# Four projections of a decoder layer in fp32: streaming the weights past stationary activations, with some blocks done in seven products

## The chip, the cores and the metric

The kernel runs on one core of a Trainium2 chip. The time is that of the device, in microseconds (us), from one launch. The engines are named as the profile names them: PE is TensorE (matmuls), PEld its weight loads, DVE is VectorE, ACT is ScalarE, POOL is GpSimd and SP is SyncE, which issues most transfers.

## The reference, cut to what matters

One layer of a hybrid decoder, 256 positions of 2048 channels, all in float32:

```
h = RMSNorm(x)
[q|k|v|lru_x|lru_gate|sc_B|sc_C|sc_x|merge_gates] = h @ W_in
A = causal attention of 8 heads, with a relative-position bias
B = RG-LRU(conv4(lru_x)) * gelu(lru_gate)
C = sc_B * conv3(sc_C * sc_x)
m = sig(g_A) * (A @ W_A) + sig(g_B) * (B @ W_B) + sig(g_C) * (C @ W_C)
x = x + m @ W_out
x = x + relu(RMSNorm(x) @ W_up)^2 @ W_down ;  final RMSNorm
```

`lru_gate`, `sc_B`, `sc_C` and `sc_x` are each 1024 columns wide. The change is about these four products and what stands beside them.

## The kernel before, in words

**Products in three parts.** Each float32 operand is cut into `hi`, its rounding to the matmul's type fp32r, and `lo`, what is left. A product is hi·hi + hi·lo + lo·hi. For weights, `in_parts` (L158) makes the cut for every 256 rows by 512 columns: ACT writes `hi` (L161), DVE subtracts to get `lo` (L162). Such a piece is a *step*. `ahead` (L165) puts the transfer and the cut of a step into the program LOOK = 3 steps before its use; there are 8 buffers for raw weights and 5 each for `hi` and `lo`.

**Two ways to run a product.** `group` (L245, entries `"ws"` of `order`) keeps the weights stationary and streams the activations: for each 128x128 piece of weights one matmul of 512 columns (`hi` against h's hi and lo side by side, L253) and one of 256 columns (`lo` against h's hi, L254). The result is transposed, channels on partitions; `total` (L351) adds its halves. 1024 columns of W_in take two groups, that is 16 steps, 128 matmuls of 512 and 128 of 256 columns. `pair` (L273, entries `"as"`) keeps the activations stationary and streams 512 columns of weights (L300): 16 steps, 192 matmuls of 512 columns for 1024 columns of W_in. Its result has positions on partitions.

**Blocks of quarters.** A pair can do some of its row blocks as a 2x2 scheme with seven products in place of eight (two row quarters by two column halves of the weights, two halves of the positions). `as_sequence` (L50) writes the order of the steps: `("s", m, ...)` is product m of a block, 6 matmuls; `("n", ...)` an ordinary step, 12 matmuls. A block takes 42 matmuls where ordinary steps take 48. It needs sums of weight quarters (four more DVE additions of 128x1024 for each block, L194), seven cuts in place of four, sums of the activations (`sums`, L94, kept in `hm` for h), and a few copies and additions of the results (`step`, L304; `other` in the evictions). NB_GATE = 2 blocks out of 4 for the gate projections `gt`, 0 for `v` and `y`, 1 for `up`.

**The order of the work.** SP's transfers are in the order of the program text; the order on the other engines is set by the tile framework's scheduler, which works from the program's order. `xr`, `q`, `k` run as groups, then `v` as a pair, then `sc` and `sx` as groups, then for each of three branches a pair `gt` and a pair `y`, twice; ahead of the second branch stands the group `sb` (function `second_factor`), ahead of the third the group `gr` (`recurrent_gate`). Smaller work is put between: `side` holds generators (`prepare`, `recurrence`, `attention`, `h_sums`), `after` holds single functions, and `a_bit` runs one function of `after` and `n` pieces of `side`. `finish` empties both; it is called ahead of the first `gt` and ahead of every `y`. GpSimd has a few tensor operations: the cut of the bias blocks `rb` (L464, L465), two multiplications in the recurrence (L516, L529), one in the gate's gelu (L675), and it issues small transfers.

Of the kernel before, what the change touches and what calls it, by code (L numbers as in the profile page):

```python
# [12 lines left out]
P = 128  # L13
# [54 lines left out]
def trunk_kernel(ctx, tc, x8, xn, pv, rows, w_in, rel, onehot, w_a, lru_w, w_l, w_s, w_out, w_up, w_down, out2):  # L68
# [53 lines left out]

    order = [("ws", w_in, g, 0, 8, 0) for g in (6, 7, 0, 1, 2, 3)]
    order.append(("as", w_in, 4, 0, 8, NB_V))
    for br, (w, gs) in enumerate(((w_a, (12, 13, 14, 15)), (w_s, (10, 11)), (w_l, (8, 9)))):
        order += [("ws", w_in, g, 0, 8, 0) for g in gs]
        for pair in range(2):
            order.append(("as", w_in, 16 + 4 * GATE[br] + 2 * pair, 0, 8, NB_GATE))
            order.append(("as", w, 2 * pair, 0, 4, NB_Y))
# [143 lines left out]
    def pair(name, w, g, plain, mix, evac, late=0):  # L273
# [42 lines left out]
        for n, s in enumerate(seq):  # L316
            u = used[0]
            used[0] += 1
            ahead(u + LOOK)
            what, m, b, gi, unit = s  # L320
            w2 = parts[u]
            if what == "n":
                held = n >= len(seq) - late
                for t in range(1 if held else 2):
                    for kk in range(2):
                        product((t, gi), n, plain(2 * unit + kk, t), w2, kk, last[t, gi] == n and kk == 1)
                keys = [(0, gi)] if held else [(0, gi), (1, gi)]
            else:
                keys = [home[m]]
                for kk in range(2):  # L330
                    product(keys[0], n, mixed(b, kk, m), w2, kk, b == nb - 1 and kk == 1)
                if b == nb - 1:
                    step(m)
            for key in keys:
                if last[key] == n and key in others:
                    rest.append(evac(*key, ps[key], got.get(others[key])))
            if n % 2:
                a_bit()
        if late:
            for n in range(len(seq) - late, len(seq)):  # L340
                for kk in range(2):
# [70 lines left out]
    def prepare():  # L412
# [42 lines left out]
        dve.tensor_copy(rsbuf, pr[:H, :384])  # L455
        rdram = dram.tile([H, 384], F32, name="rdram")
        pool.dma_start(rdram, rsbuf)
        rb = []
        for i in range(4):
            src = bass.AP(tensor=rdram.tensor, offset=rdram.offset + 2 * i * 384, ap=[[1, P], [384, 2], [1, S]])  # L460
            t = block(f"rb{i}")
            pool.dma_start(t.rearrange("p (h c) -> p h c", h=2), src)
            rb.append((block(f"rh{i}", F32R), block(f"rl{i}", F32R)))
            pool.tensor_copy(rb[i][0], t)  # L464
            pool.tensor_sub(rb[i][1], t, rb[i][0].bitcast(F32))  # L465
        for _ in range(5):
            yield
        for i in range(4):
# [7 lines left out]
    A, B, C = [], [], []  # L476
    beside(prepare())


# [23 lines left out]
    def recurrence():  # L503
        tt, aa = [], []
        for g in range(8):
            c = half(xc, g)
            pg = small(f"pg{g}")
            pe.matmul(pg[:, :S], lw[g // 4][:, (g % 4) * P:(g % 4 + 1) * P], c, start=True, stop=True)
            pe.matmul(pg[:, S:], lw[2 + g // 4][:, (g % 4) * P:(g % 4 + 1) * P], c, start=True, stop=True)
            if g % 2 == 0:  # L510
                tt.append(block(f"tt{g}"))
                aa.append(block(f"aa{g}"))
            act.activation(half(tt, g), pg[:, :S], AF.Sigmoid, bias=col(C_BA + g))
            i_ = t256(f"i{g}")
            act.activation(i_, pg[:, S:], AF.Sigmoid, bias=col(C_BX + g))
            pool.tensor_mul(c, c, i_)  # L516
            yield

        for g in range(8):
            act.activation(half(aa, g), half(tt, g), AF.Exp, scale=nsp8[:, g:g + 1])  # L520
            act.activation(half(tt, g), half(tt, g), AF.Tanh, scale=sp4[:, g:g + 1])
            if g % 4 == 3:
                yield
        for g2 in range(4):
            act.activation(tt[g2], tt[g2], AF.Sqrt)
        yield
        for g2 in range(4):
            dve.scalar_tensor_tensor(tt[g2], aa[g2], 1.0, tt[g2], op0=OP.add, op1=OP.mult)
            pool.tensor_mul(tt[g2], tt[g2], xc[g2])  # L529
            yield  # L530
        for g2 in range(4):
            hb = block(f"hb{g2}")
            for m in range(2):
                ss = slice(m * S, (m + 1) * S)
# [8 lines left out]
    for which in range(2):  # L543
        for gidx in range(2):
# [66 lines left out]
    hm = {}

    def h_sums():
        for b in range(NB_GATE):
            a = [block(f"ha{b}{i}") for i in range(2)]
            for i in range(4):
                h = hl[4 * b + i].bitcast(F32)
                dve.tensor_add(half(a, i), h[:, :S], h[:, S:])
            hm[b] = sums(f"h{b}", *a)
            yield  # L620
# [5 lines left out]
    sc = []
    for gidx in range(2):
        def evac(j, ps, gidx=gidx):
            g = 4 * gidx + j
            if g % 2 == 0:  # L630
                sc.append(block(f"sc{g}"))
            b = total(ps, f"sc{g}")
            dve.tensor_mul(half(sc, g), b, rsb)
        group(f"sc{gidx}", w_in, 12 + gidx, hl, evac)
    for gidx in range(2):
        def evac(j, ps, gidx=gidx):
            g = 4 * gidx + j
            b = total(ps, f"sx{g}")

            def rest():  # L640
                dve.tensor_mul(b, b, rsb)
                xp = t256(f"sp{g}", S + 2)
                dve.memset(xp[:, :2], 0.0)
                c = half(sc, g)
                dve.tensor_mul(xp[:, 2:], b, c)
                act.activation(c, xp[:, :S], AF.Copy, scale=col(C_SCW + g))
                for m in range(1, 3):
                    dve.scalar_tensor_tensor(c, xp[:, m:m + S], col(C_SCW + 8 * m + g), c, op0=OP.mult, op1=OP.add)
            return rest
        group(f"sx{gidx}", w_in, 14 + gidx, hl, evac)  # L650
    def second_factor():
        for gidx in range(2):
            def evac(j, ps, gidx=gidx):
                g = 4 * gidx + j
                b = total(ps, f"sb{g}")
                dve.tensor_mul(b, b, rsb)
                dve.tensor_mul(b, b, half(sc, g))
                o = block(f"C{g}", F32R)
                split(o, b)
                C.append(o)  # L660
            group(f"sb{gidx}", w_in, 10 + gidx, hl, evac)


    def recurrent_gate():
        for gidx in range(2):
            def evac(j, ps, gidx=gidx):
                g = 4 * gidx + j
                y = total(ps, f"gr{g}")

                def rest():  # L670
                    dve.tensor_mul(y, y, rsb)
                    z = t256(f"gz{g}")
                    act.activation(z, y, AF.Square)
                    act.activation(z, z, AF.Copy, scale=0.044715, bias=1.0)
                    pool.tensor_mul(z, z, y)  # L675
                    act.activation(z, z, AF.Tanh, scale=math.sqrt(2.0 / math.pi))
                    dve.scalar_tensor_tensor(y, z, 1.0, y, op0=OP.add, op1=OP.mult)
                    dve.scalar_tensor_tensor(y, half(hh, g), 0.5, y, op0=OP.mult, op1=OP.mult)
                    o = block(f"B{g}", F32R)
                    split(o, y)  # L680
                    B.append(o)
                return rest
# [278 lines left out]
```

## Time and profile before

| | us |
|---|---|
| three runs: lowest, median, highest | 1564.76, 1564.84, 1566.17 |
| the profiled execution | 1565.48 |
| its span, first to last instruction | 1563.7 |
| PE busy | 1534.1 (98%) |
| DVE busy | 1308.3 (84%) |
| ACT busy | 937.7 (60%) |
| POOL busy | 53.0 (3%) |

A busy matmul engine is not one at its peak: matmuls overlap, and the time that counts is from the start of one to the start of the next. A stage is told by its first matmul and the first of the next stage. DVE and ACT instructions overlap a little too, so the busy time of a run of equal ones is counted as a whole.

### The profile page before, as it was taken

To read this page: it belongs to the slowest core of one execution; us is meant where nothing else is said; L and a number is where in the kernel's file an instruction comes from. 1 tells how busy PE (TensorE), PEld (TensorE's weight loads), DVE (VectorE), ACT (ScalarE), POOL (GpSimd) and SP (SyncE) were. 2 spreads that over 40 slices of the span, in tenths; PEclk is the share of its full clock that TensorE was granted. 3 is DMA by queue.
4 is the path that set the end of the run, shared out by engine and by line. 5 is a ranking of instruction groups with operands and counts; after the bars stand their busy time and mean duration, and the time that the engine had idled before them with its cause. 6 is when DMAs were issued, how large, how long until landed. Compare 5 with 4: busy or idle time off the path is not lost.

```text
span 1563.7 us, 19974 instructions
## 1 busy us (share of the span) xinstructions
PE 1534.1 (98%) x7252; PEld 1276.1 (82%) x7252; DVE 1308.3 (84%) x1558; ACT 937.7 (60%) x1217; POOL 53.0 (3%) x70
## 2 busy tenths in 40 slices
PE   7999999999999999999999999999999999999997
PEld 6888888878888888777888888888888888888885
DVE  6775576998669885989899888997899789987897
ACT  6555856565546563666567666556655576656663
POOL 1021200000000000200000000000000000000000
PEclk9999999999999999999999999999999999999999
DMA  9765555475754585474765654676566664676453
GB/s 358 237 203 164 161 188 168 127 258 156 251 186 159 201 268 187 136 260 145 268 199 176 219 168 149 214 239 199 163 215 216 205 207 152 204 229 203 159 190 135
DMA packets 87572, 309.73 MB, mean 198 GB/s; under 512 B 10269, under 2 KB 10533, under 8 KB 87472
## 3 DMA queue, kind: packets, MB, share of 16 engines
q1 hardware_dynamic: 83808, 298.67, 58.1%
q0 software_dynamic: 2656, 8.45, 2.0%
q10 hardware_dynamic: 1008, 1.32, 0.3%
q8 instruction: 57, 0.93, 0.2%
q14 instruction: 43, 0.35, 0.1%
HBM read 306.30 MB, written 2.11 MB: 197 GB/s over the span
## 4 chain that ended last, share of the span: by engine, by line
PE 90%; DVE 4%; ACT 2%; DMA 2%; issue 1%; SPq 0%; DVEq 0%; ACTq 0%
PE up L300 22%; PE dn L300 20%; PE gt L300 12%; PE y L300 8%; PE wo L300 5%; PE qk L253 4%; PE v L300 3%; PE qk L254 2%; PE sc L253 2%; PE gr L253 2%; PE sx L253 2%; DMA raw<-in_w_in 2%; PE sb L253 2%; DVE lo L162 1%; ACT hi L161 1%
## 5 line engine op out<-in xcount | busy, mean ns | idle before, releaser
L161 ACT ACTIVATE hi<-raw 128x1024 fp32r<-128x1024 f32 x672 | 698.9, 1058 | 512.5 <-PE up L300 89.7
L162 DVE TENSOR_TENSOR lo<-raw,hi 128x1024 fp32r<-128x1024 f32 x672 | 807.0, 1227 | 202.1 <-ACT hi L161 188.5
L300 PE MATMUL up<-hi,h 128*128 128x512 f32 x864 | 271.2, 390 | 0.0
L194 DVE TENSOR_TENSOR raw<-raw,raw 128x1024 f32<-128x1024 f32 x160 | 194.2, 1224 | 3.0 <-DMA raw<-in_w_down 0.9
L300 PEld LDWEIGHTS up<-hi,h 128*128 128x128 f32 x864 | 161.9, 188 | 33.4
L300 PE MATMUL gt<-hi,h 128*128 128x512 f32 x528 | 167.5, 391 | 3.8 <-ACT hi L161 3.8
L300 PE MATMUL up<-lo,h 128*128 128x512 f32 x432 | 168.5, 390 | 0.0
L300 PE MATMUL dn<-hi,UH 128*128 128x512 f32 x352 | 137.3, 390 | 2.3 <-ACT UH L871 2.3
L300 PE MATMUL dn<-lo,UH 128*128 128x512 f32 x352 | 136.8, 389 | 0.0
L300 PE MATMUL dn<-hi,UL 128*128 128x512 f32 x352 | 136.1, 389 | 0.0
L300 PEld LDWEIGHTS gt<-hi,h 128*128 128x128 f32 x528 | 98.9, 188 | 25.8 <-ACT hi L161 5.3
L300 PE MATMUL gt<-lo,h 128*128 128x512 f32 x264 | 102.9, 390 | 0.0
L300 PEld LDWEIGHTS up<-lo,h 128*128 128x128 f32 x432 | 81.1, 188 | 16.6
L253 PE MATMUL qk<-h,hi 128*128 128x512 f32 x256 | 91.5, 401 | 0.0
L300 PEld LDWEIGHTS dn<-hi,UH 128*128 128x128 f32 x352 | 66.1, 188 | 16.6 <-ACT UH L871 3.2
L300 PEld LDWEIGHTS dn<-hi,UL 128*128 128x128 f32 x352 | 66.1, 188 | 14.2
L300 PEld LDWEIGHTS dn<-lo,UH 128*128 128x128 f32 x352 | 66.1, 188 | 13.6
L254 PE MATMUL qk<-h,lo 128*128 128x256 f32 x256 | 71.8, 280 | 0.0
L300 PEld LDWEIGHTS gt<-lo,h 128*128 128x128 f32 x264 | 49.6, 188 | 10.6 <-DVE lo L162 0.2
L253 PEld LDWEIGHTS qk<-h,hi 128*128 128x128 f32 x256 | 48.1, 188 | 12.2 <-ACT hi L161 0.6
L253 PE MATMUL xr<-h,hi 128*128 128x512 f32 x128 | 44.9, 407 | 8.1 <-DVE h L380 6.8
L254 PEld LDWEIGHTS qk<-h,lo 128*128 128x128 f32 x256 | 48.3, 189 | 0.3
(546 smaller groups left out, 2533.8 us busy)
## 6 DMA issues: line engine op xcount, KB each, us to landing
raw<-in_w_in SPq DMA_DIRECT2D x222, 512.0 KB, 4.3
raw<-in_w_up SPq DMA_DIRECT2D x128, 512.0 KB, 4.4
raw<-in_w_down SPq DMA_DIRECT2D x128, 512.0 KB, 4.6
raw<-in_w_out SPq DMA_DIRECT2D x32, 512.0 KB, 4.5
raw<-in_w_a SPq DMA_DIRECT2D x16, 512.0 KB, 5.2
raw<-in_w_s SPq DMA_DIRECT2D x16, 512.0 KB, 5.4
raw<-in_w_l SPq DMA_DIRECT2D x16, 512.0 KB, 5.3
gb<-in_rows POOLq DMA_DIRECT2D x12, 256.0 KB, 4.4
```

The costliest lines, as they stand in the source:

```text
L161: act.activation(hi, raw, AF.Copy)
L162: dve.tensor_sub(lo, raw, hi.bitcast(F32))
L194: dve.tensor_add(t, t, add)
L253: pe.matmul(ps[j], hi[:, kk, cs], acts[k], start=(k == 0), stop=False)
L254: pe.matmul(ps[j][:, :S], lo[:, kk, cs], acts[k][:, :S], start=False, stop=(k == nk - 1))
L300: pe.matmul(ps[key], hl_[x], w2[y][:, kk], start=key not in begun, stop=end and i == 2, skip_group_check=True)
```

## The change

The four products of `sc`, `sx`, `sb` and `gr` go from two groups each to one pair each, with 1, 1, 2 and 1 blocks of quarters. Their results now have positions on partitions, so `sx` (by then multiplied with `sc`), `sb` and `gr` are transposed on PE by the new `turned`, 16 transposes of 128x128 each. The sums of h move from `side`, behind attention, to `after`, beside `v`. `pace` while attention runs goes from 3 (once for four steps of a group) to 2 (once for two steps of a pair). GpSimd's tensor operations go to ACT and DVE. The gelu is computed on blocks of 512 columns, before the transposes.

```diff
-NB_V, NB_Y = 0, 0
+NB_GR, NB_SC, NB_SX, NB_SB, NB_V, NB_Y = 1, 1, 1, 2, 0, 0
...
-    for br, (w, gs) in enumerate(((w_a, (12, 13, 14, 15)), (w_s, (10, 11)), (w_l, (8, 9)))):
-        order += [("ws", w_in, g, 0, 8, 0) for g in gs]
+    order += [("as", w_in, 12, 0, 8, NB_SC), ("as", w_in, 14, 0, 8, NB_SX)]
+    for br, w in enumerate((w_a, w_s, w_l)):
+        if br == 1:
+            order.append(("as", w_in, 10, 0, 8, NB_SB))
+        elif br == 2:
+            order.append(("as", w_in, 8, 0, 8, NB_GR))
...
             if n % 2:
-                a_bit()
+                a_bit(pace[0])
...
+    def turned(name, o0, o1, j):
+        ps = small(name)
+        for q in range(2):
+            for th, src in ((0, o0), (1, o1)):
+                at = (2 * q + th) * P
+                pe.transpose(ps[:, at:at + P], src[:, (2 * j + q) * P:(2 * j + q + 1) * P], ident)
+        return ps
...
-            pool.tensor_copy(rb[i][0], t)
-            pool.tensor_sub(rb[i][1], t, rb[i][0].bitcast(F32))
...
+            act.activation(rb[i][0], rbt[i], AF.Copy)
+            dve.tensor_sub(rb[i][1], rbt[i], rb[i][0].bitcast(F32))
...
-            pool.tensor_mul(c, c, i_)
+            if g:
+                dve.tensor_mul(half(xc, g - 1), half(xc, g - 1), last)
+            last = i_
...
-            pool.tensor_mul(tt[g2], tt[g2], xc[g2])
+            dve.tensor_mul(tt[g2], tt[g2], xc[g2])
...
+    after += [h_sums(b) for b in range(2)]
...
-    beside(h_sums())
-    pace[0] = 3
...
-        group(f"sc{gidx}", w_in, 12 + gidx, hl, evac)
...
-        group(f"sx{gidx}", w_in, 14 + gidx, hl, evac)
+    pace[0] = 2
+    sc, scn = [None] * 4, {}
+    def evac(t, i, ps, other):
+        o = scn[t, i] = block(f"scn{t}{i}")
+        if other is not None:
+            dve.tensor_add(o, ps, other)
+            ps = o
+        act.activation(o, ps, AF.Copy, scale=rs1[:, S + t:S + t + 1])
+    pair("sc", w_in, 12, lambda k, t: in_two(hl[k], t), hm, evac)
+    def evac(t, i, ps, other):
+        o = scn[t, i]
+        if other is not None:
+            x = block(f"sx{t}{i}")
+            dve.tensor_add(x, ps, other)
+            ps = x
+        dve.scalar_tensor_tensor(o, ps, rs1[:, S + t:S + t + 1], o, op0=OP.mult, op1=OP.mult)
+        if t == 0:
+            return
+        o0 = scn[0, i]
+        def rest(j):
+            def it():
+                n = 2 * i + j
+                px = turned(f"psx{n}", o0, o, j)
+                sc[n] = block(f"sc{n}")
+                for q in range(2):
+                    g = 2 * n + q
+                    xp = t256(f"sp{g}", S + 2)
+                    dve.memset(xp[:, :2], 0.0)
+                    act.activation(xp[:, 2:], px[:, q * S:(q + 1) * S], AF.Copy)
+                    c = half(sc, g)
+                    act.activation(c, xp[:, :S], AF.Copy, scale=col(C_SCW + g))
+                    for m in range(1, 3):
+                        dve.scalar_tensor_tensor(c, xp[:, m:m + S], col(C_SCW + 8 * m + g), c, op0=OP.mult, op1=OP.add)
+            return it
+        later.extend(rest(j) for j in range(2))
+    later = []
+    pair("sx", w_in, 14, lambda k, t: in_two(hl[k], t), hm, evac)
+    after += later
...
+            def rest(j):
+                def it():
+                    n = 2 * i + j
+                    px = turned(f"psb{n}", o0, o, j)
+                    for q in range(2):
+                        g = 2 * n + q
+                        b = t256(f"sb{g}b")
+                        dve.tensor_mul(b, px[:, q * S:(q + 1) * S], half(sc, g))
+                        C[g] = block(f"C{g}", F32R)
+                        split(C[g], b)
+                return it
...
+        pair("sb", w_in, 10, lambda k, t: in_two(hl[k], t), hm, evac)
+        after.extend(later)
...
-                    pool.tensor_mul(z, z, y)
...
-            group(f"gr{gidx}", w_in, 8 + gidx, hl, evac)
...
+            act.activation(y, ps, AF.Copy, scale=rs1[:, S + t:S + t + 1])
+            z = block(f"gz{t}{i}")
+            act.activation(z, y, AF.Square, scale=math.sqrt(0.044715))
+            def inner():
+                dve.scalar_tensor_tensor(z, z, 1.0, y, op0=OP.add, op1=OP.mult)
+                act.activation(z, z, AF.Tanh, scale=math.sqrt(2.0 / math.pi))
+            def outer():
+                dve.scalar_tensor_tensor(y, z, 1.0, y, op0=OP.add, op1=OP.mult)
+            def factor(j):
+                def it():
+                    n = 2 * i + j
+                    px = turned(f"pgr{n}", grn[0, i], y, j)
+                    b = block(f"hg{n}")
+                    dve.scalar_tensor_tensor(b, px, 0.5, hh[n], op0=OP.mult, op1=OP.mult)
+                    for q in range(2):
+                        g = 2 * n + q
+                        B[g] = block(f"B{g}", F32R)
+                        split(B[g], b[:, q * S:(q + 1) * S])
+                return it
...
+        pair("gr", w_in, 8, lambda k, t: in_two(hl[k], t), hm, evac)
...
+        after.extend(later)
```

## Rows read from the trace of the kernel before

**Rows 1.** The profile's page: busy time of each engine with its share of the span and its instructions, the granted TensorE clock in 40 slices (tenths), and the chain that ended last by engine.

```profile
PE 1534.1 (98%) x7252; PEld 1276.1 (82%) x7252; DVE 1308.3 (84%) x1558; ACT 937.7 (60%) x1217; POOL 53.0 (3%) x70
...
PEclk9999999999999999999999999999999999999999
...
PE 90%; DVE 4%; ACT 2%; DMA 2%; issue 1%; SPq 0%; DVEq 0%; ACTq 0%
```

**Rows 2.** Busy time of each engine in single stages. The first column is the stretch and its length; behind PEclk stand the DMA engines' busy share and GB/s. In order: `v`; `sc`; `sx`; the first `gt`; the second `gt`; `sb`; the `gt` behind it; the `gt` after that; `gr`; the `gt` behind it; the last `gt`.

```profile
153.88:199.46 45.58, 45.58 (x203) 37.71 (x201) 27.05 (x24) 35.58 (x51) 10.38 (x7) 1.00 0.55 169
199.46:253.64 54.18, 54.18 (x317) 46.77 (x315) 36.61 (x77) 34.43 (x71) 0.00 (x0) 1.00 0.54 169
253.64:303.10 49.46, 49.46 (x287) 43.09 (x286) 42.41 (x80) 27.64 (x48) 2.21 (x4) 1.00 0.55 169
303.10:347.41 44.31, 41.83 (x182) 33.43 (x181) 42.92 (x59) 28.67 (x34) 0.00 (x0) 1.00 0.60 198
...
369.17:409.97 40.80, 40.80 (x181) 33.80 (x180) 35.71 (x36) 25.59 (x26) 0.00 (x0) 1.00 0.70 234
431.73:476.94 45.21, 45.21 (x257) 39.19 (x256) 29.60 (x42) 19.60 (x27) 0.00 (x0) 1.00 0.55 171
476.94:518.21 41.27, 41.16 (x182) 33.68 (x181) 39.70 (x47) 25.84 (x32) 1.08 (x2) 1.00 0.64 221
539.97:580.77 40.80, 40.80 (x181) 33.79 (x180) 37.10 (x38) 25.28 (x26) 0.00 (x0) 1.00 0.70 230
602.53:647.74 45.21, 45.21 (x257) 39.19 (x256) 32.80 (x45) 22.23 (x35) 2.98 (x3) 1.00 0.52 165
647.74:694.10 46.36, 42.63 (x182) 33.28 (x181) 44.71 (x53) 31.52 (x48) 6.91 (x9) 1.00 0.66 209
715.86:760.25 44.39, 43.79 (x197) 35.05 (x196) 44.07 (x52) 30.15 (x36) 4.30 (x8) 1.00 0.63 216
```

**Rows 3.** The same view for one `dn` stage, a pair with two blocks of quarters behind the pair `up` with one.

```profile
1127.47:1211.72 84.25, 83.68 (x377) 69.21 (x376) 80.07 (x80) 51.66 (x56) 0.00 (x0) 1.00 0.61 203
```

**Rows 4.** PE in order of time (start, duration) in a group: one 512-column and one 256-column matmul, and the next.

```profile
59.97 0.40 PE L253 MATMUL qk<-h,hi 128*128 128x512 f32 x1
60.21 0.28 PE L254 MATMUL qk<-h,lo 128*128 128x256 f32 x1
60.33 0.40 PE L253 MATMUL qk<-h,hi 128*128 128x512 f32 x1
```

**Rows 5.** The chain that ended last, in order of time: a `gt` stage without a gap, and eight transposes between matmuls of a later pair.

```profile
369.33 40.80 PE gt L300 x180
...
1087.62 0.87 PE pu L869 x8
```

**Rows 6.** What PE waited for in the `gt` stages behind `sx` and behind `gr` (in brackets the idle time before the matmul, and what ended it).

```profile
320.28 0.73 PE L300 MATMUL gt<-hi,h 128*128 128x512 f32 x2 [1.56 <-ACT hi L161]
...
665.01 0.49 PE L300 MATMUL gt<-hi,h1ch 128*128 128x512 f32 x1 [1.52 <-ACT hi L161]
```

**Rows 7.** DVE in order of time, runs of equal instructions (start, duration of the run).

```profile
562.53 4.63 DVE L162 TENSOR_TENSOR lo<-raw,hi 128x1024 fp32r<-128x1024 f32 x4
567.08 1.28 DVE L702 TENSOR_TENSOR gt<-gt,gt 128x512 f32<-128x512 f32 x2
568.28 1.41 DVE L704 SCALAR_TENSOR_TENSOR gt<-gt,rs,gb 128x512 f32<-128x512 f32 x2
...
486.42 3.49 DVE L194 TENSOR_TENSOR raw<-raw,raw 128x1024 f32<-128x1024 f32 x3
...
306.23 2.07 DVE L648 SCALAR_TENSOR_TENSOR sc<-sp,pvt,sc 128x256 f32<-128x256 f32 x5
...
475.88 0.42 DVE L356 TENSOR_TENSOR sb5b<-sb,sb5a 128x256 f32<-128x256 f32 x1
476.22 0.41 DVE L657 TENSOR_TENSOR sb4b<-sb4b,sc 128x256 f32<-128x256 f32 x1
```

**Rows 8.** DVE at the end of the `y` stage ahead of the last `gt`, in order of time.

```profile
707.15 1.22 DVE L162 TENSOR_TENSOR lo<-raw,hi 128x1024 fp32r<-128x1024 f32 x1
708.40 1.23 DVE L194 TENSOR_TENSOR raw<-raw,raw 128x1024 f32<-128x1024 f32 x1
709.54 1.22 DVE L162 TENSOR_TENSOR lo<-raw,hi 128x1024 fp32r<-128x1024 f32 x1
710.68 1.22 DVE L194 TENSOR_TENSOR raw<-raw,raw 128x1024 f32<-128x1024 f32 x1
711.81 1.22 DVE L162 TENSOR_TENSOR lo<-raw,hi 128x1024 fp32r<-128x1024 f32 x1
712.95 2.48 DVE L194 TENSOR_TENSOR raw<-raw,raw 128x1024 f32<-128x1024 f32 x2
```

**Rows 9.** DVE and POOL in order of time in the `gt` stage behind `gr`.

```profile
655.88 1.75 DVE L162 TENSOR_TENSOR lo<-raw,hi 128x1024 fp32r<-128x1024 f32 x1
...
657.89 1.21 DVE L162 TENSOR_TENSOR lo<-raw,hi 128x1024 fp32r<-128x1024 f32 x1
...
655.63 0.92 POOL L675 TENSOR_TENSOR gz<-gz,gr5b 128x256 f32<-128x256 f32 x1 [1.04 <-DVE gr3b L678]
```

More of the change, by code (lines that the diff above doesn't have):

```diff
@@ L457, in prepare @@
         pool.dma_start(rdram, rsbuf)
-        rb = []
+        rb, rbt = [], []
         for i in range(4):
@@ L462, in prepare @@
             pool.dma_start(t.rearrange("p (h c) -> p h c", h=2), src)
+            rbt.append(t)
             rb.append((block(f"rh{i}", F32R), block(f"rl{i}", F32R)))
-            pool.tensor_copy(rb[i][0], t)
-            pool.tensor_sub(rb[i][1], t, rb[i][0].bitcast(F32))
-        for _ in range(5):
+            if i % 2:
+                yield
+        for _ in range(4):
             yield
+        for i in range(4):
+            act.activation(rb[i][0], rbt[i], AF.Copy)
+            dve.tensor_sub(rb[i][1], rbt[i], rb[i][0].bitcast(F32))
+        yield
         for i in range(4):
@@ L474, in prepare @@
             yield
-    A, B, C = [], [], []
+    A, B, C = [], {}, {}
     beside(prepare())
@@ L521, in recurrence @@
             act.activation(half(tt, g), half(tt, g), AF.Tanh, scale=sp4[:, g:g + 1])
+            if g == 0:
+                dve.tensor_mul(half(xc, 7), half(xc, 7), last)
             if g % 4 == 3:
@@ L551, in trunk_kernel, with h_sums, rest @@
             group(f"qk{which}{gidx}", w_in, 2 * which + gidx, hl, evac)
-    vv = {}
+    vv, hm = {}, {}
+    def h_sums(b):
+        def rest():
+            a = [block(f"ha{b}{i}") for i in range(2)]
+            for i in range(4):
+                h = hl[4 * b + i].bitcast(F32)
+                dve.tensor_add(half(a, i), h[:, :S], h[:, S:])
+            hm[b] = sums(f"h{b}", *a)
+        return rest
+    after += [h_sums(b) for b in range(2)]
     def evac(t, i, ps, other):
@@ L610, in trunk_kernel @@
     beside(attention())
[L611 to L620, printed above, removed]
-    beside(h_sums())
-    pace[0] = 3
[L626 to L633, printed above, removed]
-        group(f"sc{gidx}", w_in, 12 + gidx, hl, evac)
@@ L635, in trunk_kernel @@
[L635 to L649, printed above, removed]
-        group(f"sx{gidx}", w_in, 14 + gidx, hl, evac)
@@ L651, in second_factor @@
-    def second_factor():
[L652 to L661, printed above, removed]
-    def recurrent_gate():
[L665 to L674, printed above, removed]
-                    pool.tensor_mul(z, z, y)
[L676 to L682, printed above, removed]
-            group(f"gr{gidx}", w_in, 8 + gidx, hl, evac)
@@ new lines, in trunk_kernel, with evac @@
+    later = []
+    pair("sx", w_in, 14, lambda k, t: in_two(hl[k], t), hm, evac)
+    after += later
+    def second_factor():
+        sbn = {}
+        def evac(t, i, ps, other):
+            o = sbn[t, i] = block(f"sbn{t}{i}")
+            if other is not None:
+                dve.tensor_add(o, ps, other)
+                ps = o
+            act.activation(o, ps, AF.Copy, scale=rs1[:, S + t:S + t + 1])
+            if t == 0:
+                return
+            o0 = sbn[0, i]
+            def rest(j):
[9 more added lines that the diff above has]
+                return it
+            later.extend(rest(j) for j in range(2))
+        later = []
+        pair("sb", w_in, 10, lambda k, t: in_two(hl[k], t), hm, evac)
+        after.extend(later)
@@ new lines, in recurrent_gate, with evac @@
+    def recurrent_gate():
+        grn, later = {}, []
+        def evac(t, i, ps, other):
+            y = grn[t, i] = block(f"gr{t}{i}")
+            if other is not None:
+                dve.tensor_add(y, ps, other)
+                ps = y
+            act.activation(y, ps, AF.Copy, scale=rs1[:, S + t:S + t + 1])
[17 more added lines that the diff above has]
+                return it
+            at = len(later)
+            later.extend([inner, outer])
+            if t:
+                later.extend(factor(j) for j in range(2))
+        pair("gr", w_in, 8, lambda k, t: in_two(hl[k], t), hm, evac)
+        for n in range(len(later) - 1):
+            if later[n].__name__ == "outer" and later[n + 1].__name__ == "inner":
+                later[n], later[n + 1] = later[n + 1], later[n]
+        after.extend(later)
```

## The prediction, made before the changed kernel ran

> **What bounds the kernel now.** I read the page first: PE is busy 98% of the span, at the full granted clock in every slice, and 90% of the chain that ended last is PE [rows 1]. That is an average, so I went on to the stages from 154 to 760 us, which the change touches. Where a stage has no stall its length is its matmuls: 180 matmuls of 512 columns in 40.80 us, 0.2267 us each [rows 5], and the two `gt` stages that stand at 40.80 have nothing else in them [rows 2]. Where a stage is longer, DVE is the reason. The `gt` behind `sx` takes 44.31 us, the one behind `sb` 41.27, the one behind `gr` 46.36: 3.51, 0.47 and 5.56 above 40.80, and DVE is busy for nearly all of them [rows 2]. PE there waits for a cut (`hi` or `lo`) that comes late [rows 6]. So the bound is PE's stream of matmuls, and at each entry into blocks of quarters DVE for a few us. A change is worth what it takes from PE, less what it adds to DVE at those entries.
>
> **Part 1: the matmuls.** In a group a pair of matmuls (512 and 256 columns) takes 60.33 − 59.97 = 0.36 us [rows 4]; over the whole stage, 45.21 us for `sb` and for `gr` [rows 2], or 0.353 us for each of 128 pairs. With activations stationary, 1024 columns without blocks are 192 matmuls, 192 × 0.2267 = 43.5 us (`v`, which has 45.58 with recurrence matmuls between [rows 2]). Each block takes 6 matmuls off, 1.36 us: 42.17 us with one block, 40.80 with two. Before: 4 × 45.21 = 180.8 us (for `sc` and `sx` the sum of both stages, 103.64, is 90.4 of this and 13.2 of attention's own matmuls, which stay). After: 3 × 42.17 + 40.80 = 167.3. **−13.5 us.**
>
> **Part 2: the transposes.** 48 new ones; eight of the same shape take 0.87 us between matmuls [rows 5], 0.109 each: **+5.2 us**. They stand on the path, since PE has no slack.
>
> **Part 3: DVE at the entries into quarters.** Back to back, a cut (`lo`) costs 1.14 us on DVE, a sum of raw weights 1.14, an operation on 128x512 0.60 (0.66 for the three-operand form), one on 128x256 0.335, and the convolution's 0.40 (differences between starts) [rows 7]. A pair with two blocks needs, through its 13th step, 13 cuts, six raw sums and one subtraction of `step`: 22.3 us. PE reaches the 13th step after 9 short steps of 1.36 and 3 of 2.72 us, 20.4 us. DVE enters with a lead: 4 cuts done (4.6 us), or with 3 to 4 raw sums as well when the stage before left it time (four cuts and four raw sums stand in the last us of `y` [rows 8]; three of those sums count, 8.0 us in all). The stall is what DVE has to do besides, plus 22.3, minus lead, minus 20.4 and the transposes. This agrees with what is known. Behind `sx`, four `rest` functions (1.5 us each): 22.3 + 6.0 − 4.6 − 20.4 = 3.3, measured 3.51. Behind `gr`, four (1.34 each) and 2.7 lost to GpSimd (below): 5.4, measured 5.56. The last `gt`, with 9.8 us of extra DVE work and 16 transposes (1.75) but the large lead: 22.3 + 9.8 − 8.0 − 22.15 = 1.95, measured 44.39 − 40.80 − 1.75 = 1.84 [rows 2].
>
> Now the same sum for the changed kernel. *Behind `sx`*: `finish` runs all four functions at once, 7.0 us on DVE (16 convolution steps of 0.40 and the memsets), plus the eviction of `sx`'s last half, 0.60 + 2 × 0.66 = 1.9; transposes 1.75. 22.3 + 8.9 − 22.15 = 9.05, minus lead: 4.45 to 1.05. *Behind `sb`*: four functions with two multiplications and two cuts each (1.34), and 0.6 of eviction: 6.15 minus lead, 1.55 to 0. *Behind `gr`*: the twelve functions are spread over the whole stage, so I count the stage: 39.8 for the pair, four `inner` and four `outer` at 0.66, four `factor` at 1.33, and 0.6: 51.0 − 42.55 of PE = 8.45, minus lead, 3.85 to 0.45. The lead after the change comes from the tail of a pair, ordinary steps of 2.72 us in which DVE needs 1.14, as in `y`, but with evictions in it; I take the middle: 2.7, 0.8 and 2.2.
>
> *Inside `sc`* there is a fourth entry that had none. One block only, but the last seven pieces of the recurrence (four scan pairs of 1.2, three times 1.26) and the first heads of attention (1.6 us of DVE per head) now fall into 19 steps. Through `s7` I count about 28.5 us of DVE against 21.8 of PE and a lead of 4.6: a stall of 2, or none with raw sums ahead; I take 1.0. `sx` has 16 steps' worth of slack for the rest of attention (22.5 against 27 with its lead).
>
> One more wait: the transposes behind `sx` follow the eviction directly. The nearest row is `dn` behind `up`, which loses 84.25 − 81.60 − 1.75 = 0.9 us in that way [rows 3]. I add 0.9 there, and 0.5 for the last `factor`, which `finish` runs just ahead of `y`.
>
> Stalls after: 2.7 + 0.8 + 2.2 + 1.0 + 1.4 = 8.1; before 9.5: **−1.4 us.**
>
> **Part 4: what moves off GpSimd.** While GpSimd multiplies in the stage behind `gr`, a cut on DVE takes 1.75 us in place of 1.21 [rows 9], 0.54 longer; five DVE instructions there were hit, 2.7 us. That is gone and is in the sum above. The Trainium skill, in "SBUF — State Buffer", section "Who interferes with whom", says that the two engines share a port as an exclusive lock, and that the loser waits for the other's whole instruction. By that rule each hit would cost up to GpSimd's 0.92 us and not 0.54; five hits would be 4.6, and 1.9 us more would come back, 1553.2 in place of 1555.1. The trace shows the smaller number, so the sum goes by it.
>
> The eight multiplications of 128x256 and four of 128x512 that DVE takes over fall into `k`, `v` and the head of `sc`, and the bias blocks' cuts (four on ACT, four on DVE) into `k`. In `v` DVE is busy 27.05 of 45.58 us [rows 2]. The sums of h (2 × 3.8 us of DVE) go there too: 27 + 7.6 + 2.4 = 37 of 45.6, so nothing is exposed. Uncovered, they would cost up to 10 us. ACT gains 15 cuts and some copies, about 13 us over 580, and stays under 75% in each stage; nothing. The weights' bytes and SP's order of transfers stay as they are; the DMA engines' share is 0.54 to 0.70 in these stages [rows 2]. GpSimd's queue keeps only its small transfers.
>
> **Sum.** −13.5 + 5.2 − 1.4 = −9.7 us. The profiled execution took 1565.48 us (span 1563.7), so 1555.8; the median of the runs is 0.64 lower: **1555.1 us.** With all bounds of part 3 at their low end the stalls are 1.5 and the time 1548.5; at their high end 13.2 and 1560.
>
> **The rivals.**
> *A, DVE always has its lead and the stalls vanish.* For it: `up` to `dn` shows only 0.9 us of loss [rows 3]. Against it: every other entry with work of an eviction behind it shows a loss. −8.3 − 9.5 = −17.8: 1547.
> *B, DVE becomes the bound at the entries.* Net, DVE gets some 38 us more work in these stages. If the scheduler leaves it three cuts of lead (3.4 us) and no raw sum, the four entries stall 5.65, 2.75, 5.05 and 2, with 1.4 as above 16.9: −8.3 + 7.4 = −0.9, 1564. For it: DVE is already busy 42 to 45 us in the stages concerned [rows 2]. Against it: the tails give it time.
> *C, slower: the shared blocks run out.* `block` hands out NBLK = 45 tiles. At the start of `sc` I count 44 live: 16 of h, 8 of q and k, 4 biases, 4 of v, and 12 of the recurrence, which is two pieces further behind than before (`prepare` has two more yields). An eviction of `sc` that finds no block holds ACT, the cuts stand behind it, and PE follows; release comes with the next `a_bit`, up to 4.1 us. It decides from the fourth such wait (16.4 us against 9.7 + 3.1): 1571. Against it: each `a_bit` frees about one block, and the evictions need one every two or three steps.
> That the change would not do what it says can only be so in part 1, if streaming weights cost more than 0.2267 per matmul; `v` and `gt` do just that already.
>
> **How the numbers follow.** Forecast (1548.5 to 1560) 0.64, A 0.06, B 0.20, C 0.10. The likeliest gives 1555. The range leaves out A and C and reaches to B's 1564: 1548.5 to 1564. 0.2%, 3.1 us, is about what a measurement of this kernel tells from no change. Faster than 1561.7: forecast, A and a third of B, 0.76; within 0.2%: the rest of B, 0.14; slower: C, 0.10.
>
> **What would show it.** `sb` near 40.8 and `gr` near 42.2 us; `sc` and `sx` together near 98.5 with attention's 13; 48 more transposes of 0.109; the `gt` stages behind them at about 46, 43.4 and 45; no DVE cut above 1.25 us; on POOL only transfers. PE waiting for a cut inside `sc` or `sx` would mean B; ACT idle for a DVE of the recurrence with PE idle behind it, C. I am wrong if streamed matmuls take longer beside so many DVE operations, or if the transposes wait for more than their eviction.

## The result, and the profile after

The changed kernel takes 1553.89 us (median; 1552.88 to 1554.71). The kernel before, run beside it, took 1565.51. The ratio is 0.9919, 95% interval 0.9907 to 0.9931, that is 11 to 15 us less. Forecast were 1555.1 and −9.7 us.

The page of the changed kernel: busy time of each engine, the granted clock in 40 slices, and the chain that ended last by engine.

```profile
PE 1527.6 (98%) x7014; PEld 1266.1 (82%) x7014; DVE 1335.6 (86%) x1557; ACT 951.7 (61%) x1213; POOL 21.5 (1%) x42
...
PEclk9999999999999999999999999999999999999999
...
PE 92%; DVE 4%; ACT 2%; issue 1%; DMA 1%; DVEq 0%; SPq 0%; ACTq 0%
```

Beside [rows 1] the bound has not moved: PE is busy for the same share of a span that is 10.7 us shorter. DVE has 27 us more to do, and POOL has lost its cuts and multiplications. The changed kernel was profiled a second time, among the experiments; its span was 1551.5 us there, and the difference of 1.5 us between the two is a stretch at half clock, shown below.

The same stages as in [rows 2], now of the changed kernel (first profile; busy time of each engine with the number of instructions, then PEclk, the DMA engines' share and GB/s). In order: `v`, `sc`, `sx`, the `gt` behind it, `sb`, the `gt` behind it, `gr`, the `gt` behind it, `y`, the last `gt`.

```profile
151.59:199.00 47.41, 47.41 (x210) 39.23 (x209) 33.06 (x47) 34.99 (x54) 0.00 (x0) 1.00 0.49 151
199.00:247.95 48.95, 48.45 (x224) 39.72 (x223) 44.46 (x73) 32.65 (x57) 0.00 (x0) 1.00 0.56 177
247.95:298.83 50.88, 50.88 (x246) 42.43 (x245) 40.59 (x67) 32.37 (x57) 1.10 (x2) 1.00 0.57 175
298.83:341.49 42.66, 42.37 (x192) 34.47 (x190) 41.14 (x51) 30.24 (x43) 1.07 (x2) 1.00 0.65 214
...
425.81:466.61 40.80, 40.80 (x182) 33.79 (x180) 37.52 (x37) 25.59 (x26) 0.00 (x0) 1.00 0.64 208
466.61:509.38 42.77, 42.77 (x197) 35.29 (x196) 40.73 (x51) 28.03 (x36) 1.08 (x2) 1.00 0.65 215
...
593.70:635.86 42.16, 42.16 (x187) 34.92 (x186) 36.15 (x38) 24.75 (x28) 0.00 (x0) 1.00 0.62 199
635.86:680.43 44.57, 42.79 (x197) 35.34 (x196) 42.37 (x48) 31.28 (x41) 1.07 (x2) 1.00 0.70 225
680.43:703.96 23.53, 23.53 (x96) 19.29 (x97) 17.06 (x21) 8.41 (x10) 0.00 (x0) 0.93 0.40 142
703.96:749.08 45.12, 43.88 (x197) 35.09 (x196) 44.31 (x52) 30.25 (x36) 4.28 (x8) 1.00 0.65 224
```

Put beside [rows 2] this is where the time went (us; `y` behind the third branch's first `gt` is 21.76 in the chain of before, as every undisturbed `y`):

| stretch | before | forecast | after, first profile | second profile |
|---|---|---|---|---|
| `sc`, `sx` and the `gt` behind | 147.95 | 144.7 | 142.49 | 142.41 |
| `sb` and the `gt` behind | 86.48 | 84.1 | 83.57 | 83.55 |
| `gr`, the `gt` behind and `y` | 113.33 | 109.2 | 110.26 | 108.66 |
| the last `gt` | 44.39 | 44.4 | 45.12 | 45.16 |
| sum | 392.15 | 382.4 | 381.44 | 379.78 |

`v` is 1.83 us longer and `q`, `k` 1.71 shorter (97.79 to 96.08): eight matmuls of the recurrence now fall into `v`, because `prepare` has two more pieces. Sums of h and DVE's new multiplications cost `v` nothing: PE is busy for all of its 47.41 us. `sc` and `sx` together take 99.83 us where the prediction's sign said 98.5; 0.87 of the difference is eight of the transposes, which run in `sx` already.

The lead of DVE at the entry into the `gt` behind `sx` (DVE of the changed kernel in order of time; the stage begins at 298.83):

```profile
289.71 2.49 DVE L198 TENSOR_TENSOR raw<-raw,raw 128x1024 f32<-128x1024 f32 x2
292.11 1.22 DVE L166 TENSOR_TENSOR lo<-raw,hi 128x1024 fp32r<-128x1024 f32 x1
293.37 1.23 DVE L198 TENSOR_TENSOR raw<-raw,raw 128x1024 f32<-128x1024 f32 x1
294.51 1.22 DVE L166 TENSOR_TENSOR lo<-raw,hi 128x1024 fp32r<-128x1024 f32 x1
295.64 1.22 DVE L198 TENSOR_TENSOR raw<-raw,raw 128x1024 f32<-128x1024 f32 x1
...
300.97 6.43 DVE L680 SCALAR_TENSOR_TENSOR sc<-sp,pvt,sc 128x256 f32<-128x256 f32 x16
```

Four raw sums of the next pair stand ready 2 us before the stage begins, with four of its cuts, and then the convolution's 16 steps run in one piece. With 8.0 us of lead the forecast's sum gave a stall of 1.05 there; the stage has 42.66 − 40.80 − 0.87 = 0.99.

The same place in the kernel before, where the stage begins at 303.10:

```profile
293.80 1.22 DVE L162 TENSOR_TENSOR lo<-raw,hi 128x1024 fp32r<-128x1024 f32 x1
295.05 2.48 DVE L194 TENSOR_TENSOR raw<-raw,raw 128x1024 f32<-128x1024 f32 x2
298.08 2.36 DVE L162 TENSOR_TENSOR lo<-raw,hi 128x1024 fp32r<-128x1024 f32 x2 [0.55 <-ACT hi L161]
...
300.70 1.22 DVE L194 TENSOR_TENSOR raw<-raw,raw 128x1024 f32<-128x1024 f32 x1
```

Three cuts and three raw sums are done ahead, 6.8 us, and not four cuts and no sum, 4.6, as the prediction had it. PE's last wait behind `sx` is also not at the 13th step but in the ninth, at the 62nd matmul of the stage, in both kernels: at 320.28 before [rows 6], and after here:

```profile
314.34 0.50 PE L304 MATMUL gt<-lo,h0ch 128*128 128x512 f32 x1 [0.23 <-DVE lo L166]
```

The one wait of PE from 635 to 700 us, and the granted clock behind it (stretches of the first profile, columns as above):

```profile
680.43 0.50 PE L304 MATMUL y<-hi,B 128*128 128x512 f32 x1 [1.78 <-ACT B L117]
```

```profile
660.00:677.00 17.00, 17.00 (x77) 14.08 (x76) 15.63 (x18) 9.59 (x12) 0.54 (x1) 1.00 0.86 278
677.00:680.00 3.00, 1.65 (x12) 1.24 (x10) 3.00 (x6) 2.19 (x4) 0.54 (x1) 1.00 0.94 344
680.00:682.00 2.00, 1.57 (x7) 1.31 (x8) 2.00 (x4) 0.69 (x2) 0.00 (x0) 0.98 1.02 418
682.00:684.00 2.00, 2.00 (x6) 1.58 (x5) 1.09 (x3) 0.72 (x2) 0.00 (x0) 0.50 0.83 277
684.00:686.00 2.00, 2.00 (x7) 1.57 (x6) 0.00 (x0) 0.81 (x1) 0.00 (x0) 0.67 0.19 76
686.00:690.00 4.00, 4.00 (x19) 3.28 (x18) 2.02 (x2) 1.31 (x2) 0.00 (x0) 1.00 0.27 101
```

`y` waits 1.78 us for B, and in this execution the clock then stands at 0.50, the 1.2 GHz level, for some 3.5 us; `y` takes 23.53 us in place of 21.76. In the second profile the same wait of 1.78 us is there, `y` has a clock of 1.00 and takes 21.93 us.

### The profile page after: what moved, and what is told of

The parts are those of the page before. It is cut to its first block, busy times and chain, and to the rows that moved or that the text cites. A ratio compares the mean times of both kernels' runs of the same rounds, so it can differ in the third digit from the quotient of the medians.

```text
span 1553.0 us, 19433 instructions
## 1 busy us (share of the span) xinstructions
PE 1527.6 (98%) x7014; PEld 1266.1 (82%) x7014; DVE 1335.6 (86%) x1557; ACT 951.7 (61%) x1213; POOL 21.5 (1%) x42
## 4 chain that ended last, share of the span: by engine, by line
PE 92%; DVE 4%; ACT 2%; issue 1%; DMA 1%; DVEq 0%; SPq 0%; ACTq 0%
PE up L304 22%; PE dn L304 20%; PE gt L304 13%; PE y L304 8%; PE wo L304 5%; PE qk L257 4%; PE v L304 3%; PE sx L304 3%; PE gr L304 3%; PE sb L304 3%; PE xr L257 2%; PE qk L258 2%; DVE lo L166 2%; PE sc L304 1%; PE xr L258 1%
## 5 line engine op out<-in xcount | busy, mean ns | idle before, releaser
L165 ACT ACTIVATE hi<-raw 128x1024 fp32r<-128x1024 f32 x687 | 716.9, 1059 | 501.6 <-PE up L304 89.7
L166 DVE TENSOR_TENSOR lo<-raw,hi 128x1024 fp32r<-128x1024 f32 x687 | 821.4, 1221 | 179.2 <-ACT hi L165 164.8
L198 DVE TENSOR_TENSOR raw<-raw,raw 128x1024 f32<-128x1024 f32 x180 | 218.5, 1221 | 2.7 <-DMA raw<-in_w_out 0.5
```

Source lines behind the costliest of these rows:

```text
L165: act.activation(hi, raw, AF.Copy)
L166: dve.tensor_sub(lo, raw, hi.bitcast(F32))
L198: dve.tensor_add(t, t, add)
```

## Experiments

The theory: the gain is PE's. The stream of matmuls is 13.5 us shorter, transposes give 5.2 back, and the stalls at the entries into quarters hang on DVE's lead. Rival 1: the gain comes from freeing DVE (no GpSimd, sums of h elsewhere). Rival 2: the transposes are hidden. Rival 3: only PE counts. Each run has a ratio to the kernel before on the same chip; as the changed kernel stands at 0.9919 and 0.9914 in two series, 0.001 of a ratio is 1.6 us. The interval of a ratio is some 2 us to either side, so differences of 3 us between two runs rest on their stages as much as on their medians. The change of `pace` was not run by itself. The change's own mark in the second series:

> The changed kernel unaltered, as the mark for the runs beside it: 1553 to 1555. If the half clock behind the wait for the last B comes and goes from execution to execution, the times fall into two heaps some 1.7 us apart.

Measured 1553.11 us (1552.86 to 1553.83), ratio 0.9914 (0.9900 to 0.9927). The four times of this series lie in one heap. Those of the first lay at 1552.9 and 1553.2, with a mean clock of 0.998, and at 1554.6 and 1554.7, with 0.997 and 0.996; only the last of these was profiled, so for the other the half clock is not shown.

**1. The small edits alone**, in the kernel before:

```diff
-            pool.tensor_mul(c, c, i_)
+            if g:
+                dve.tensor_mul(half(xc, g - 1), half(xc, g - 1), last)
+            last = i_
...
+    after += [h_sums(b) for b in range(2)]
...
-    beside(h_sums())
...
-                    pool.tensor_mul(z, z, y)
+                    dve.tensor_mul(z, z, y)
```

The cuts of `rb` and the multiplications of `tt` leave GpSimd as in the change.

> The kernel before with only the small edits: no tensor operation on GpSimd, and the sums of h beside v. The four products stay groups. Theory (the matmul stream carries the gain): only the 2.7 us that GpSimd's multiplications cost the cuts behind gr come back, about 1562.5 in place of 1565.2. Rival 1 (the gain comes from the entries into quarters, where DVE is freed): most of the 11.6 us is here already, 1558 or less.

Measured 1567.75 against 1567.48 us, ratio 1.0003 (0.9993 to 1.0012). No gain, so rival 1 falls, and so does the 2.7 us of the theory. The stage behind `gr` (stretch, busy times):

```profile
648.30:697.33 49.03, 44.56 (x182) 35.65 (x181) 44.00 (x59) 31.30 (x48) 0.54 (x1) 0.93 0.59 189
```

It takes 49.03 us against 46.36 [rows 2], part of it at half clock: PE is busy 1.93 us longer, and idle for 4.47 us in place of 3.73. The multiplications that left GpSimd are now DVE's, eight of 0.335 us, 2.7 in all, and stand in the same chain ACT, DVE, ACT, DVE; freeing DVE from GpSimd gives back no more than that costs.

**2. No quarters in the four new pairs.**

```diff
-NB_GR, NB_SC, NB_SX, NB_SB, NB_V, NB_Y = 1, 1, 1, 2, 0, 0
+NB_GR, NB_SC, NB_SX, NB_SB, NB_V, NB_Y = 0, 0, 0, 0, 0, 0
```

> The changed kernel with no block of quarters in sc, sx, sb and gr (activations still stationary). Theory: 5 blocks times 6 matmuls times 0.2267 us, 6.8 us more of PE, less 1 to 2 us of stalls that go with DVE's 20 raw sums and 15 cuts: 1559 to 1561. Rival 1: DVE is what counts, so without that work it is 1554 or faster.

Measured 1556.83 us, ratio 0.9935 (0.9922 to 0.9947): 2.5 to 3.3 us more than the changed kernel, about half of the theory's 5 to 6.8, and not rival 1's gain. The stages `sb`, `gr`, the `gt` behind `gr`, the `y` behind that and the last `gt`:

```profile
427.62:471.14 43.52, 43.52 (x194) 36.04 (x193) 25.15 (x22) 18.94 (x19) 0.00 (x0) 1.00 0.54 164
...
598.72:642.24 43.52, 43.52 (x193) 36.04 (x192) 28.68 (x28) 21.57 (x24) 0.00 (x0) 1.00 0.57 169
642.24:684.78 42.54, 42.54 (x197) 35.32 (x196) 39.66 (x44) 28.82 (x36) 0.54 (x1) 1.00 0.68 217
684.78:706.67 21.89, 21.89 (x100) 18.11 (x98) 19.25 (x24) 10.34 (x14) 0.54 (x1) 1.00 0.57 191
706.67:751.01 44.34, 43.75 (x197) 35.05 (x196) 44.06 (x52) 30.17 (x36) 4.29 (x8) 1.00 0.63 219
```

The matmuls cost what was said (43.52 in place of 40.80 and 42.16). But the `gt` behind `gr` is down to its matmuls and transposes, 40.80 + 1.74 = 42.54: the wait for B is gone, and the last `gt` is 0.8 shorter. In `sc` and `sx` only 0.8 of 2.7 us is lost, since their excess over matmuls and transposes (2.3 us with the `gt` behind, in the changed kernel) shrinks to 1.0. Quarters are worth 6.8 us on PE, and some 3 net.

Here stands also what the forecast had wrong about the cause: streaming the weights alone is worth 10 us, made up of 6.8 less for matmuls and 5.2 more for transposes. The rest, some 8 us, is stalls behind `sx` and `gr` that are gone. One part of that can be counted: ahead of a `gt` a pair leaves DVE with four cuts and four raw sums done, a group with three and three, 2.3 us at each entry. The rest, most of it behind `gr`, is not taken apart.

**3. The wait for B, taken away in two ways.** With quarters, `as_sequence` ends a pair with the first column half (`n1`), so B0 to B3 come last, and `y` begins with them; without quarters the second half comes last. Once by letting `y` begin with the other half:

```diff
-            seq = as_sequence(nu, nb, n == last_pair, w is w_down)
+            seq = as_sequence(nu, nb, n == last_pair, w is w_down or w is w_l)
```

> The changed kernel in which the two pairs y of the third branch take their row blocks in the order 2, 3, 0, 1, so that they begin with B4 to B7, which the gate's list makes first; nothing else is moved and the DVE work lies where it was. Theory (y waits because a pair with quarters ends with the first column half, so that B0 to B3 come last, and y begins with them): the 1.78 us wait goes, and the last gt, which began late with its cuts, is back at 44.4: 2.5 us less than the changed kernel, 1550.5. Rival: DVE is behind by then whatever y asks for first: at most 1 us less.

and once by a shorter list:

```diff
-            later.extend([inner, outer])
+            later.append(inner)
+            outers.append(outer)
             if t:
+                i0, i1 = later.pop(-2), later.pop(-1)
+                o0, o1 = outers[-2:]
+                later.extend([lambda: (i0(), i1()), lambda: (o0(), o1())])
                 later.extend(factor(j) for j in range(2))
```

> The changed kernel with the gate's two inner functions run as one and its two outer ones as one, so that the list behind gr has 8 entries and not 12 and is through before the gt pair ends; the same instructions. Theory: the wait of 1.78 us for the last B at the entry of y goes, and with it the stretch at half clock behind it (1.77 us, in the executions that show it): 1550.5 to 1552. Rival: the same DVE work comes earlier and stalls the gt pair by as much: 1554.

Measured 1550.39 us, ratio 0.9897 (0.9882 to 0.9913), and 1550.37 us, ratio 0.9896 (0.9882 to 0.9909): 2.7 us less in both than the changed kernel in its second series (by the first series' ratio 3.4 and 3.6). With the other half first, the `gt` behind `gr`, `y`, and the last `gt`:

```profile
636.65:679.19 42.54, 42.54 (x197) 35.34 (x196) 40.35 (x45) 29.25 (x37) 0.54 (x1) 1.00 0.67 217
679.19:701.08 21.89, 21.89 (x99) 18.13 (x98) 19.25 (x24) 10.34 (x14) 0.54 (x1) 1.00 0.54 192
701.08:745.42 44.34, 43.73 (x197) 35.07 (x196) 44.06 (x52) 30.14 (x36) 4.29 (x8) 1.00 0.64 217
```

2.03 us less in the first, 0.8 in the last, ahead of which DVE's cuts and sums now come in the order and at the times of the kernel before (three cuts and four sums, in place of four and three). That moving no DVE work at all gives the same gain shows that the wait hangs on which half `y` asks for first, and not on the amount of DVE work. Either one beats both kernels.

**4. Every new transpose twice.**

```diff
-        for q in range(2):
+        for q in (0, 1, 0, 1):
```

> The changed kernel with every one of the 48 new transposes issued twice into the same place. Theory: transposes stand on the path, 48 times 0.109 us: 5.2 us more, 1559. Rival 2: they run in time that PE loses anyway at the entries behind sx, sb and gr: at most 1.5 us more.

Measured 1556.63 us, ratio 0.9933 (0.9921 to 0.9945): 2.2 to 3.0 us, between theory and rival. By stages against the second profile: `sx` and the `gt` behind it +1.3 (52.93 + 41.91 against 50.87 + 42.64), the `gt` behind `sb` +1.67 (44.42), the one behind `gr` +0.85 (45.42), together 3.85, within the intervals of the ratios. Where the stage has hardly a stall (behind `sb`) the 16 cost 1.67, nearly their full 1.74; where it has one, they run partly inside it.

**5. Two blocks of quarters everywhere.**

```diff
-NB_GR, NB_SC, NB_SX, NB_SB, NB_V, NB_Y = 1, 1, 1, 2, 0, 0
+NB_GR, NB_SC, NB_SX, NB_SB, NB_V, NB_Y = 2, 2, 2, 2, 0, 0
```

> The changed kernel with 2 blocks of quarters in sc, sx and gr too (sb has 2 already). PE has 3 times 1.36 = 4.1 us less. Theory with DVE's bound at the entries: sc with the recurrence and attention beside it needs about 34 us of DVE through its 13th step against 22 of PE and a lead of 5 to 8, so 4 us or more are lost there and 1 to 3 in sx: 1554 to 1558. Rival 3 (only PE's stream counts): 1550.

Measured 1553.28 us, ratio 0.9917 (0.9903 to 0.9930): as the changed kernel, a little under the theory's 1554 to 1558 and well above rival 3's 1550. The stage `sc`:

```profile
199.02:251.37 52.35, 49.96 (x230) 39.40 (x228) 51.47 (x81) 37.27 (x67) 0.00 (x0) 1.00 0.50 168
```

DVE is busy 51.47 of 52.35 us and PE misses 2.4: DVE's bound, as the theory has it for `sc`. In `sx`, where the theory had 1 to 3 us lost, PE misses nothing (busy for all of 47.97 us). With the gate's merged list and two blocks in `gr` alone:

```diff
-NB_GR, NB_SC, NB_SX, NB_SB, NB_V, NB_Y = 1, 1, 1, 2, 0, 0
+NB_GR, NB_SC, NB_SX, NB_SB, NB_V, NB_Y = 2, 1, 1, 2, 0, 0
```

> gate_merged with two blocks of quarters in gr too. PE has 1.36 us less in gr. Theory: the tail of gr still gives DVE its full lead, so the gt pair behind it loses at most 0.5 more: 0.9 to 1.4 us less than gate_merged, 1549.2. Rival (DVE's bound at the entry): the two stalls cancel, 1550.4 or more.

Measured 1550.48 us, ratio 0.9900 (0.9886 to 0.9913). `gr` is 40.80 us, and the `gt` with the `y` behind it 65.99 in place of 64.47: what PE gives, the entry takes. The rival was right.

**6. The gate's product as groups again**, its code as before with DVE in GpSimd's place:

```diff
-            order.append(("as", w_in, 8, 0, 8, NB_GR))
+            order += [("ws", w_in, g, 0, 8, 0) for g in (8, 9)]
```

> The changed kernel with the recurrent gate's product as two groups again (its gelu on 256 columns, all on ACT and DVE, nothing on GpSimd). Theory: gr 45.21 in place of 42.16 us (+3.05), 16 transposes less (-1.75), the wait of 1.8 us at the entry of y gone, the entry of gt behind it about 2.5 us late: +1 to +3 us, 1555 to 1557. Rival 1: the same time as the changed kernel or less, since DVE has less to do.

Measured 1558.51 us, ratio 0.9952 (0.9938 to 0.9965): 5 to 6 us more, beyond the forecast. `gr` +3.05, and the `gt` behind it:

```profile
639.17:686.97 47.80, 43.36 (x182) 34.78 (x181) 43.90 (x59) 31.31 (x48) 0.54 (x1) 0.96 0.62 193
```

47.80 us without transposes, 3.2 more than with the pair and its 16; PE waits there 2.76 us once, and the clock falls. So at this entry the group form's chain costs more than the count of DVE's work said.

**7. GpSimd's share back** (the bias blocks' cuts and the recurrence's multiplications):

```diff
-            act.activation(rb[i][0], rbt[i], AF.Copy)
-            dve.tensor_sub(rb[i][1], rbt[i], rb[i][0].bitcast(F32))
+            pool.tensor_copy(rb[i][0], rbt[i])
+            pool.tensor_sub(rb[i][1], rbt[i], rb[i][0].bitcast(F32))
...
-                dve.tensor_mul(half(xc, g - 1), half(xc, g - 1), last)
+                pool.tensor_mul(half(xc, g - 1), half(xc, g - 1), last)
...
-                dve.tensor_mul(half(xc, 7), half(xc, 7), last)
+                pool.tensor_mul(half(xc, 7), half(xc, 7), last)
...
-            dve.tensor_mul(tt[g2], tt[g2], xc[g2])
+            pool.tensor_mul(tt[g2], tt[g2], xc[g2])
```

> The changed kernel with the bias blocks' cuts and the recurrence's twelve multiplications back on GpSimd. Theory: they fall into k, v and the head of sc, where DVE has slack; 0 to 1 us more, 1554 to 1555. Rival 1: DVE blocked by GpSimd shows again at the entry of sc, which now has quarters: 3 us more or worse.

Measured 1554.87 us, ratio 0.9923 (0.9910 to 0.9935), 0.6 to 1.4 us more, which these intervals hardly tell from none. The stages do: `sc` 50.92 us in place of 48.90. DVE and POOL at its entry:

```profile
193.80 0.69 DVE L550 SCALAR_TENSOR_TENSOR tt<-aa,tt 128x512 f32<-128x512 f32 x1
...
195.00 1.79 DVE L550 SCALAR_TENSOR_TENSOR tt<-aa,tt 128x512 f32<-128x512 f32 x1
196.72 1.77 DVE L550 SCALAR_TENSOR_TENSOR tt<-aa,tt 128x512 f32<-128x512 f32 x1
198.41 2.31 DVE L166 TENSOR_TENSOR lo<-raw,hi 128x1024 fp32r<-128x1024 f32 x1
...
202.89 1.21 DVE L166 TENSOR_TENSOR lo<-raw,hi 128x1024 fp32r<-128x1024 f32 x1
...
194.63 7.25 POOL L551 TENSOR_TENSOR tt<-tt,xc 128x512 f32<-128x512 f32 x4 [13.94 <-DVE tt L550]
```

GpSimd's four multiplications end at 201.88. While they run, a cut takes 2.31 us, behind them 1.21; the three-operand form takes 1.79 and 1.77 beside them, 0.69 ahead of them. Each grows by 1.1 us, whatever its own length. The theory and the rival each had a part: `q` and `k` cost 0.4 us, `v` nothing, the entry of `sc` 2 us.

**8. The lead, by the program.** `LOOK` sets how many steps ahead a cut stands in the program.

```diff
-LOOK = 3
+LOOK = 2
```

> The changed kernel with the cuts put into the program two steps before their use and not three. Theory (the entries hang on DVE's lead): one cut and its raw sum less of lead, 1.1 to 2.3 us more at each entry that already stalls (sc, gt behind sx, gt behind gr, the last gt, wo), 5 to 10 us more: 1558 to 1563. Rival (the stalls come from something else, a chain behind one eviction): at most 1 us more.

Measured 1559.66 us, ratio 0.9957 (0.9945 to 0.9970): 6 to 7 us more, as the theory says in sum. By stages only three of its five places: `sc`, the last `gt` and `wo`.

```profile
199.19:249.27 50.08, 49.23 (x224) 39.54 (x223) 47.75 (x75) 33.23 (x59) 0.00 (x0) 1.00 0.56 179
703.53:751.60 48.07, 45.79 (x197) 36.47 (x196) 44.49 (x52) 30.46 (x36) 4.29 (x8) 0.96 0.63 219
773.36:863.48 90.12, 87.35 (x402) 71.72 (x401) 86.36 (x99) 60.23 (x83) 0.00 (x0) 1.00 0.57 188
```

Of the 2.9 us that the last `gt` loses, 1.8 is PE busy for longer at a mean clock of 0.96. The `gt` stages behind `sx`, `sb` and `gr` keep their times to 0.1 us (42.62, 42.70, 44.57): behind `sx` DVE has the same four cuts and four raw sums done with `LOOK` = 2, so the scheduler gathers this lead whatever `LOOK` is. Why it is otherwise at the other three entries is not shown.

```diff
-LOOK = 3
+LOOK = 4
```

> The changed kernel with the cuts four steps ahead. Theory: up to one cut more of lead where the five buffers for the parts allow it; 0 to 3 us less: 1550 to 1553. Rival: evictions and the functions of after stand behind one more cut in DVE's and ACT's order, and the banks of PSUM come free later: 1 us more or worse.

Measured 1554.71 us, ratio 0.9929 (0.9916 to 0.9941), 1.6 to 2.3 us more, as the rival says. `sc`, the last `gt` and `wo` gain 0.5, 0.6 and 0.9 us, but the `gt` behind `sb` goes from 42.75 to 43.51, and each of the four `dn` stages loses about 1 us (84.25 to 85.2 in the first three). That one of the evictions stands behind the extra cut there, as the rival has it, is not shown.

## Why the prediction was right

*Part 1, matmuls: right to 0.1 us.* `sb` 40.80, `gr` 42.16, both forecast. Experiments 1 and 2 show that the pairs carry the change: without them nothing is gained, with them and without quarters 10 us are. They do not show that the matmuls alone carry it. Of the 12.4 us between the kernel before and the second profile, matmuls less transposes are 8.3, as forecast, and stalls the other 4.

*Part 2, transposes: the price is right, the place only partly.* 16 cost 1.74 us where nothing else is late; behind `sx` and `gr` part of them lies inside a wait (experiment 4).

*Part 3, stalls: the term that was mis-sized.* Forecast 8.1 us after, 9.5 before. In the second profile they are 2.3 in `sc`, `sx` and the `gt` behind them (forecast 4.6), 0.2 behind `sb` (0.8), 2.2 behind `gr` with `y` (2.7), and 0.8 new in the last `gt` (none): 5.5, and so −4.0 where −1.4 was said. Taking the middle of the lead failed: at the three entries behind pairs it is at its high end, 8.0 us by the prediction's count of four cuts and three sums. With 8.0 the same sum gives 1.05 behind `sx` (measured 0.99) and 0.45 on DVE behind `gr` (0.25 above matmuls, transposes and the wait). In the profiled run 1.6 us at half clock hide part of this, so that its −10.7 looks nearer to −9.7 than the parts are.

The sum itself was less tested than the prediction says. Behind `sx` in the kernel before it gave 3.3 for 3.51 with a lead of 4.6; with the 6.8 that stood ready it gives 1.1, and the step in which PE waits last is the ninth and not the 13th. For the last `gt`, [rows 8] show three cuts and four sums ahead of the stage, and not four cuts: again 6.8 counted in the same way, which gives 3.1 for 1.84. So its agreement with the kernel before was in part luck, and that with 0.99 after may be too.

*The last `factor` ahead of `y`:* I gave it 0.5 us; it cost 1.78, 0.8 more in the last `gt`, and in the first profile 1.6 at half clock. The mechanism was named, its cause was not: quarters turn round the order in which B is finished.

*Part 4, GpSimd: no gain at the gate.* The 2.7 us of contention at `gr` [rows 9] were real, but doing the same multiplications on DVE costs as much (experiment 1). What the change gained behind `gr` came from the pair, not from GpSimd's absence. In the recurrence the contention would have cost 2 us at the new entry of `sc` (experiment 7). I had put those multiplications down at nothing, which is what they cost on DVE; that they would have cost something where they were I had not said.

*By the Trainium skill, "SBUF — State Buffer", section "Who interferes with whom"*, the loser of the shared port waits for the other's whole instruction. The rows come near to that, and the prediction, which held 0.54 against 0.92 us, read them wrongly: the 0.92 has GpSimd's own wait for DVE in it. Undisturbed, such a multiplication of 128x256 takes 0.74 us (at 169.48 in the kernel before) and one of 128x512 that starts ahead of DVE 1.28 us (at 173.96); beside them DVE's instructions grow by 0.54 [rows 9] and by 1.1 us (experiment 7).

*Rivals.* A (all stalls gone) is nearer than I gave it: 5.5 of 9.5 us are left, and 2.8 of these hang on one order of halves. B is real one block further on: with two blocks in `sc` DVE is busy 51.47 of 52.35 us. C, the blocks running out, left no trace: the one wait of PE in `sc` above 0.25 us is 0.49 us for an operation of attention.

## What to carry to other kernels

Count a stage's entry apart from its average: what DVE must do through the step at which PE waits last, less the lead that the stage before lets it gather. Read both from the rows, the step from PE's last wait and the lead from the cuts and sums that stand ready before the entry: a sum that agrees with a measured stall proves nothing while its lead is assumed. When a reordered product finishes its halves in another order, look at which half its consumer asks for first; turning the consumer round cost nothing and gave 2.7 us here. Moving an operation off a contending engine pays only when the engine that takes it over has slack at that place.

## What the runs showed of the hardware that I had not expected

Short waits of PE can bring the granted clock down to 0.50 for some 3 us or more behind them, and not in every execution. The wait of 1.78 us for B is in five profiles (both of the changed kernel, experiment 7 and both of experiment 8), and the clock fell behind it in one. PE had been busy 1.65 of the 3.00 us ahead in that one, and just as long in the second profile, where it stayed at 1.00. Behind 2.07 us in experiment 5 it stayed at 1.00 too. In experiments 1 and 6, with waits of 2.79 and 2.76 us and one of 1.28 close behind, the stage's mean clock was 0.93 and 0.96. With `LOOK` = 2 three waits of 0.25, 0.44 and 0.81 us stood close together ahead of some 3 us at 0.50 in the last `gt`; in the kernel before, in the stages of [rows 6] with waits of 1.56 us and less, it was 1.00.
